# Output product: half of the last pass by split weights, two-bank PSUM tiles, and a set order of transposes and norms

## The chip, the cores and the metric

The kernel runs on one core of one Trainium2 chip. The metric is device time in microseconds for one execution. The kernel before was timed in three runs: 2250.57, 2253.21 and 2257.24 us, median 2253.21.

## The reference

A trunk of two layers works on an input of 1024 tokens with 1024 features, all in float32. Layer 0 mixes with attention, layer 1 with a gated recurrence. Behind each mixer stand an output projection with a norm and a residual, and then a gated feed-forward product:

```python
def rmsnorm(x, g):
    xf = x.astype(jnp.float32)
    y = xf * lax.rsqrt(jnp.mean(xf * xf, axis=-1, keepdims=True) + RMS_EPS)
    return (y * g.astype(jnp.float32)).astype(x.dtype)

def swiglu(h, w_gate, w_up, w_down):
    return (jax.nn.silu(h @ w_gate) * (h @ w_up)) @ w_down

    for layer in range(DEPTH):
        ...
            m = attention_mixer(h, attn_w_in[j], attn_rel_bias[j], attn_w_out[j])
        ...
        x = x + rmsnorm(m, norm_mix_post[layer])
        h = rmsnorm(x, norm_ffn_pre[layer])
        f = swiglu(h, ffn_w_gate[layer], ffn_w_up[layer], ffn_w_down[layer])
        x = x + rmsnorm(f, norm_ffn_post[layer])
```

The mixer ends with a product by `w_out` (1024 x 1024). That product, `norm_mix_post`, the residual, `norm_ffn_pre` and the start of the gate product are what this case is about.

## The kernel before

Most products run in float32r on operands split into a high part and the rest (`hi`, `lo`): three products hi x hi, lo x hi and hi x lo are added in PSUM. A product of plain float32 operands, without a split, is one instruction that shows as two records in the trace.

The output product `out_product` runs once per layer. It takes the 1024 tokens in eight tiles of 128. The weights are eight blocks (`kt`) of 128 x 1024. Tiles 0 to 2 are the first pass and tiles 3 to 5 the second: for each `kt` the weights are loaded, split by ScalarE (hi) and VectorE (lo), the activations likewise, and each tile gets 2 halves x 3 products of 128 x 512. Tiles 6 and 7 are the last pass: all eight weight blocks are loaded again into the eight buffers with the tag `w`, and used plain, with plain activations (16 instructions per tile).

Behind a tile's product stands its chain of small steps, in `post_norm`, `rstd` and `pre_norm`: VectorE multiplies the PSUM halves by the gain into `mg` (L223); ScalarE squares the halves into `junk` with a sum (L175); GpSimd adds the two sums (L177), scales and adds epsilon (L178) and raises to -0.5 (L179); VectorE forms the new residual `x` (L226); ScalarE squares it, GpSimd works out its factor, ScalarE scales `x` into `mg` (L200); TensorE transposes it in eight instructions (L208); and `HiddenS.take` copies the two PSUM tiles (ScalarE, L85), forms four differences `tf` (VectorE, L89) and splits everything into `hS` (ScalarE hi, L96; VectorE lo, L89).

The feed-forward's gate and up products (`gate_up`) use Strassen's scheme: seven products per block with combinations of weight quarters (A11, A12, A22, S1 to S4, held split in `q`) and combinations of the transposed activations (`hS`). A token tile fills 64 of the 512 columns of `hS` (`cols` in `HiddenS.take`). The first gate block is computed in two halves of the columns: `early`, 0 to 256, which tiles 0 to 3 fill, and `late`, 256 to 512, which tiles 4 to 7 fill. Each half has 7 x 4 x 3 = 84 products of 128 x 256 (L549 to L551). The first up product, with 512 columns, follows.

The order on each engine is found when the kernel is built: a scheduler with estimated times takes the instruction that is ready first, within what the buffers of the pools allow. `tc.issue_after(i)` keeps an instruction behind another in that order. DMAs are issued by SP in its own order; a DMA waits there for its buffer. PSUM has eight banks of 512 float32 per partition: six single-bank tiles (`mm`) and two for transposes (`tr`).

## Time and profile before

| | |
|---|---|
| median of three runs | 2253.21 us |
| profiled execution, own time | 2252.08 us |
| its span on the core | 2250.3 us |
| mean granted TensorE clock | 0.992 of 2.4 GHz |
| TensorE, VectorE, ScalarE, GpSimd busy | 98%, 68%, 51%, 10% |
| output product, layer 0: first product, last pass, first up product | 511.15, 580.09, 640.55 us |
| output product, layer 1: last pass, first up product | 1558.68, 1616.98 us |

Times are counted from the start of the span. The profile gives each engine's busy time; because matmuls are pipelined, a record of a matmul is longer than the distance to the next one, so costs on TensorE are read from start to start. "Idle before" is the time in which the engine had nothing running ahead of an instruction, with the instruction that ended it. A wait on an engine other than TensorE costs only if TensorE waits for it later.

### The profile page before, as it was taken

The page shows a single profiled execution, that of the slowest core. Times are in us where ns is not written, and L with a number is a line of the kernel's source. Part 1 is how long each engine was busy: PE and PEld are TensorE (multiplying, and loading weights), DVE is VectorE, ACT ScalarE, POOL GpSimd, SP SyncE. Part 2 cuts the span into 40 slices and gives each one's busy share as a digit, 9 for nine tenths or more (in the row PEclk, how much of TensorE's full clock was granted, in tenths as well). Part 3 has the DMA queues.
Part 4 walks back from the last instruction along what each step waited for, and adds up shares of the span by engine and source line. Part 5 has one row for each costly group of instructions (what it writes and reads, how often), then busy time and mean ns, then how long its engine had stood idle before and what let it go on. Part 6 is the DMA issues. An engine that isn't in the chain of part 4 may idle for free. (4 is left out here: it accounts for less than half of the span.)

```text
span 2250.3 us, 30764 instructions
## 1 busy us (share of the span) xinstructions
PE 2204.5 (98%) x11166; PEld 1804.5 (80%) x11166; DVE 1537.2 (68%) x2504; ACT 1146.9 (51%) x2132; POOL 220.5 (10%) x474
## 2 busy tenths in 40 slices
PE   8999999999999999999999999999999999999997
PEld 8888888878678888888887777887788888888875
DVE  5776765464677767676867677436887767769665
ACT  4545455465765454432536576537755454425433
POOL 2111212131100000000001232102000000000010
PEclk9999999999999999999999999999999999999998
DMA  5101011125623323245558511358233323337466
GB/s 171 44 29 34 24 43 46 55 98 156 223 85 113 116 90 122 89 131 183 173 157 255 141 57 47 95 183 273 71 117 108 122 90 116 96 117 264 130 206 187
DMA packets 187132, 273.13 MB, mean 121 GB/s; under 512 B 13922, under 2 KB 115298, under 8 KB 186979
## 3 DMA queue, kind: packets, MB, share of 16 engines
q1 hardware_dynamic: 186338, 269.06, 38.1%
q10 hardware_dynamic: 640, 2.10, 0.3%
q8 instruction: 88, 1.44, 0.3%
q14 instruction: 66, 0.53, 0.1%
HBM read 205.57 MB, written 65.54 MB: 120 GB/s over the span
## 5 line engine op out<-in xcount | busy, mean ns | idle before, releaser
L549 PE MATMUL ps<-hS,q 128*128 128x512 f32 (+1 forms) x1288 | 490.5, 382 | 3.0 <-ACT hS L96 2.9
L550 PE MATMUL ps<-hS,q 128*128 128x512 f32 (+1 forms) x1288 | 490.6, 381 | 0.2 <-DVE hS L89 0.2
L551 PE MATMUL ps<-hS,q 128*128 128x512 f32 (+1 forms) x1288 | 489.1, 381 | 0.0
L530 DVE TENSOR_TENSOR q<-raw,q 128x512 fp32r<-128x512 f32 x308 | 204.4, 686 | 180.8 <-ACT q L529 180.4
L549 PEld LDWEIGHTS ps<-hS,q 128*128 128x128 f32 x1288 | 242.8, 189 | 50.1 <-ACT hS L96 4.1
L550 PEld LDWEIGHTS ps<-hS,q 128*128 128x128 f32 x1288 | 243.7, 189 | 47.2 <-DVE hS L89 0.7
L551 PEld LDWEIGHTS ps<-hS,q 128*128 128x128 f32 x1288 | 243.6, 189 | 45.8
L529 ACT CAST q<-raw 128x512 fp32r<-128x512 f32 x308 | 176.9, 615 | 157.3 <-DVE raw L538 137.1
L630 PE MATMUL ps<-o,o 128*128 128x512 f32 x616 | 241.2, 392 | 2.4 <-DVE o L625 2.3
L631 PE MATMUL ps<-o,o 128*128 128x512 f32 x616 | 238.6, 392 | 0.5 <-DVE o L741 0.5
L629 PE MATMUL ps<-o,o 128*128 128x512 f32 x616 | 222.0, 395 | 8.9 <-ACT o L740 5.9
L518 ACT ACTIVATE raw<-raw,gcol 128x256 f32<-128x256 f32 x352 | 150.2, 498 | 157.2 <-DMA raw<-in_ffn_w_up_dram 83.1
L624 ACT CAST o<-raw 128x512 fp32r<-128x512 f32 x206 | 123.9, 621 | 197.2 <-PE ps L631 60.5
L625 DVE TENSOR_TENSOR o<-raw,o 128x512 fp32r<-128x512 f32 x206 | 137.9, 688 | 66.2 <-ACT o L624 65.2
L178 POOL TENSOR_SCALAR rs<-ss 128x1 f32<-128x1 f32 x64 | 30.2, 472 | 1266.5 <-ACT junk L175 1169.1
L629 PEld LDWEIGHTS ps<-o,o 128*128 128x128 f32 x616 | 116.4, 189 | 37.7 <-ACT o L740 8.0
L155 DVE TENSOR_TENSOR wlo<-raw,whi 128x1024 fp32r<-128x1024 f32 x76 | 92.9, 1223 | 67.5 <-ACT whi L154 66.4
L630 PEld LDWEIGHTS ps<-o,o 128*128 128x128 f32 x616 | 116.4, 189 | 28.0 <-DVE o L625 3.9
L631 PEld LDWEIGHTS ps<-o,o 128*128 128x128 f32 x616 | 116.3, 189 | 24.9 <-DVE o L741 0.9
L154 ACT CAST whi<-raw 128x1024 fp32r<-128x1024 f32 x76 | 79.8, 1052 | 53.0 <-PE ps L166 20.2
L369 ACT COPY pt<-tr 128x512 f32<-128x512 f32 (+1 forms) x128 | 65.5, 527 | 78.9 <-PE tr L365 78.3
L165 PE MATMUL psq<-hT,whi 128*128 128x512 f32 x256 | 101.2, 395 | 1.1 <-DVE v L264 1.1
(194 smaller groups left out, 4281.1 us busy)
## 6 DMA issues: line engine op xcount, KB each, us to landing
raw<-in_ffn_w_down_dram SPq DMA_DIRECT2D x96, 256.0 KB, 4.3
raw<-in_ffn_w_gate_dram SPq DMA_DIRECT2D x44, 512.0 KB, 4.2
raw<-in_ffn_w_up_dram SPq DMA_DIRECT2D x44, 512.0 KB, 4.4
gS<-c SPq DMA_DIRECT2D x88, 256.0 KB, 3.7
raw<-gS SPq DMA_DIRECT2D x88, 256.0 KB, 2.9
gA<-c SPq DMA_DIRECT2D x66, 256.0 KB, 3.3
raw<-in_attn_w_in_dram SPq DMA_DIRECT2D x24, 512.0 KB, 4.1
raw<-in_attn_w_out_dram SPq DMA_DIRECT2D x24, 512.0 KB, 4.2
```

The costliest lines, as they stand in the source:

```text
L165: nc.tensor.matmul(ps, wh[:, kt, cols], hh[:, kt, :], start=kt == 0, stop=False)
L518: nc.scalar.activation(raw[:, i], raw[:, i], AF.Copy, scale=gain[:, 4 * k + i:4 * k + i + 1])
L529: self.last = nc.scalar.copy(t[:, 0], src).ins
L530: nc.vector.tensor_tensor(t[:, 1], src, t[:, 0].bitcast(F32), op=ALU.subtract)
L549: nc.tensor.matmul(ps, a[:, 0, kt, :], bh, start=kt == 0, stop=False)
L550: nc.tensor.matmul(ps, a[:, 0, kt, :], bl, start=False, stop=False)
L551: nc.tensor.matmul(ps, a[:, 1, kt, :], bh, start=False, stop=kt == 3)
L624: nc.scalar.copy(t[:, 0], src)
L625: tt(t[:, 1], src, t[:, 0].bitcast(F32), op=ALU.subtract)
L629: nc.tensor.matmul(ps, a[0], b[:, 0], start=first, stop=False)
L630: nc.tensor.matmul(ps, a[0], b[:, 1], start=False, stop=False)
L631: nc.tensor.matmul(ps, a[1], b[:, 0], start=False, stop=last)
```

## The change

Six things change, all around the output product of both layers.

- In the last pass the split weights of the last four `kt` of the second pass are kept (`kept`), and tiles 6 and 7 are multiplied by them with split activations, in three products each. Only the first four `kt` are loaded again and used plain. Their `w` buffers are those of the kept weights.
- A tile's product stands in one PSUM tile of two banks (three such buffers), so that the gain product, and the square, are one instruction of 1024 elements. Transposes have a pool of their own, and the feed-forward opens its pool behind the output product.
- `rstd` scales by D^-0.5 within the square; the sums of two parts are chained, so that GpSimd has one instruction fewer behind the last square.
- `post_norm` is cut in two: for each of the first two passes the three gain products and squares are issued first, then the rest of each tile.
- The transposes and takes of tiles 3 to 7 are put in a set order by `behind`, that is by `issue_after`.
- The first gate block's weights are loaded and split from within the output product, in another order (A22 third); the last three splits, S3, S1 and S4, stand behind the norm of tile 6. Products S2 and A22 of the early half stand behind the transposes of tiles 6 and 7.

```diff
         ss = [pool.tile([P, 1], F32, tag="ss", bufs=4, name=self.uid("ss")) for _ in parts]
-        for p, o in zip(parts, ss):
-            self.squared = nc.scalar.activation(junk, p, AF.Square, accum_out=o).ins
-        if len(parts) == 2:
-            nc.gpsimd.tensor_tensor(ss[0], ss[0], ss[1], op=ALU.add)
-        nc.gpsimd.tensor_scalar(rs, ss[0], 1.0 / D, EPS, op0=ALU.mult, op1=ALU.add)
+        eps = EPS
+        for i, (p, o) in enumerate(zip(parts, ss)):
+            self.squared = nc.scalar.activation(junk, p, AF.Square, scale=D ** -0.5, accum_out=o).ins
+            if i < len(parts) - 1:
+                nc.gpsimd.tensor_scalar(o, o, eps, None, op0=ALU.add)
+                eps = o
+        nc.gpsimd.tensor_scalar(rs, ss[-1], eps, None, op0=ALU.add)
         nc.gpsimd.tensor_tensor(rs, rs, self.neghalf, op=ALU.pow)
...
+    @contextmanager
+    def behind(self, instructions):
+        with ExitStack() as c:
+            for i in instructions:
+                c.enter_context(self.tc.issue_after(i))
+            yield
...
-            nc.scalar.activation(h, x, AF.Copy, scale=rs)
+            self.scaled = nc.scalar.activation(h, x, AF.Copy, scale=rs).ins
...
+                self.turned[t] = nc.tensor.transpose(
+                    ps[:, j * P:(j + 1) * P], h[:, kt * P:(kt + 1) * P], self.ident).ins
             pst.append(ps.rearrange("p (a b) -> p a b", a=4))
+        if later:
+            return lambda: sink.take(t, pst, h, pool)
         sink.take(t, pst, h, pool)
...
+    def post_norm_of(self, ms, mg, x_src, x_dst, t, gpost, sink, pool, x=None):
         nc = self.nc
-        x = pool.tile([P, D], F32, tag="nx", bufs=2, name=self.uid("x"))
+        if x is None:
+            x = pool.tile([P, D], F32, tag="nx", bufs=2, name=self.uid("x"))
         for d, s in rows(t, x_src):
             self.load(x[d, :], s)
         junk = pool.tile([P, D // len(ms)], BF16, tag="junk", bufs=1, name=self.uid("junk"))
         if mg is ms[0][1]:
             rs = self.rstd(pool, [m for _, m in ms], junk)
         for c, m in ms:
-            nc.vector.tensor_tensor(mg[:, c], m, gpost[:, c], op=ALU.mult)
+            scaled = nc.vector.tensor_tensor(mg[:, c], m, gpost[:, c], op=ALU.mult).ins
         if mg is not ms[0][1]:
             rs = self.rstd(pool, [m for _, m in ms], junk)
-        nc.vector.scalar_tensor_tensor(x, mg, rs, x, op0=ALU.mult, op1=ALU.add)
-        for k, (d, s) in enumerate(rows(t, x_dst)):
-            (nc.scalar if k and sink is None else nc.sync).dma_start(s, x[d, :])
-        if sink is not None:
-            self.pre_norm(pool, x, mg, None, sink, t, self.psum_t)
+        self.last_m = [self.squared, scaled]
+        def rest(later=False):
+            nc.vector.scalar_tensor_tensor(x, mg, rs, x, op0=ALU.mult, op1=ALU.add)
+            for k, (d, s) in enumerate(rows(t, x_dst)):
+                (nc.scalar if k and sink is None else nc.sync).dma_start(s, x[d, :])
+            if sink is not None:
+                return self.pre_norm(pool, x, mg, None, sink, t, self.psum_t, later)
+        return rest
...
+        def psum():
+            return pp.tile([P, D], F32, tag="mm", bufs=3, name=self.uid("ps"))
         def matmuls(ps, passes, first, last):
             for n in range(2):
                 for i, (x, y) in enumerate(passes):
-                    nc.tensor.matmul(ps[n], x, y[:, n, :], start=first and i == 0,
+                    nc.tensor.matmul(ps[:, n * 512:(n + 1) * 512], x, y[:, n, :], start=first and i == 0,
                                      stop=last and i == len(passes) - 1)
         def norm(t, ps):
             mg = ap.tile([P, D], F32, tag="mg", bufs=3, name=self.uid("mg"))
-            ms = [(slice(i * 512, (i + 1) * 512), p) for i, p in enumerate(ps)]
-            self.post_norm(ms, mg, x_src, x_dst, t, gpost, sink, ap)
-        gpost = None
+            x = self.apool.tile([P, 1152], F32, tag="first", name=self.uid("x"))[:, :D] if t in (2, 5) else None
+            return self.post_norm_of([(slice(0, D), ps)], mg, x_src, x_dst, t, gpost, sink, ap, x)
+        def split_act(a, ah, al):
+            nc.scalar.copy(ah, a)
+            nc.vector.tensor_tensor(al, a, ah.bitcast(F32), op=ALU.subtract)
+        gpost, kept = None, []
         for t0 in (0, 3):
-            pst = [[self.psum() for _ in range(2)] for _ in range(3)]
+            pst = [psum() for _ in range(3)]
             for kt in kts:
-                pool, bufs = (self.apool, 1) if t0 == 0 and kt == kts[0] else (ap, 3)
-                a = act(kt, t0, 3, pool, bufs)
+                if t0 == 0 and kt == kts[0]:
+                    a, ah, al = self.apool.tile([P, 1152], F32, tag="first", name=self.uid("first")).rearrange(
+                        "p (a b) -> a p b", a=3)
+                    ah, al = ah.bitcast(F32R), al.bitcast(F32R)
+                    nc.sync.dma_start(a, aT[kt][:, 0:3 * P])
+                else:
+                    a = act(kt, t0, 3, ap, 3)
+                    ah, al = (ap.tile([P, 384], F32R, tag=n, bufs=3, name=self.uid(n)) for n in ("ah", "al"))
                 wh, wl = self.split(wv[kt], 2, 512)
-                ah, al = (pool.tile([P, 384], F32R, tag=n, bufs=bufs, name=self.uid(n)) for n in ("ah", "al"))
-                nc.scalar.copy(ah, a)
-                nc.vector.tensor_tensor(al, a, ah.bitcast(F32), op=ALU.subtract)
+                kept = kept[-3:] + [(wh, wl)]
+                split_act(a, ah, al)
                 for t in range(3):
                     tok = slice(t * P, (t + 1) * P)
                     matmuls(pst[t], [(ah[:, tok], wh), (ah[:, tok], wl), (al[:, tok], wh)],
                             kt == kts[0], kt == kts[-1])
             if gpost is None:
                 gpost = self.gain(ap, "gpost", gpost_v)
-            for t in range(3):
-                norm(t0 + t, pst[t])
+            rests = [norm(t0 + t, pst[t]) for t in range(3)]
+            for rest in rests[:2]:
+                rest()
+            take = rests[2](t0 > 0)
+        pst = [psum() for _ in range(2)]
+        for i, (kt, (wh, wl)) in enumerate(zip(kts[4:], kept)):
+            a = act(kt, 6, 2, ap, 3)
+            ah, al = (ap.tile([P, 384], F32R, tag=n, bufs=3, name=self.uid(n))[:, :2 * P] for n in ("ah", "al"))
+            split_act(a, ah, al)
+            for t in range(2):
+                tok = slice(t * P, (t + 1) * P)
+                matmuls(pst[t], [(ah[:, tok], wh), (ah[:, tok], wl), (al[:, tok], wh)], i == 0, False)
         rows, acts = [], []
-        for i, kt in enumerate(kts):
+        for i, kt in enumerate(kts[:4]):
             raw = self.main.tile([P, 2, 512], F32, tag="w", bufs=8, name=self.uid("raw"))
             nc.sync.dma_start(raw, wv[kt])
             rows.append(raw)
-            acts.append(act(kt, 6, 2, ap, 3, ("act", "ah", "al")[i % 3]))
+            acts.append(act(kt, 6, 2, ap, 3, ("act", "act", "act", "ah")[i]))
+        turned = {(0, 0): 3, (0, 2): 4, (1, 0): 5}
         for t in range(2):
-            ps = [self.psum() for _ in range(2)]
-            for i in range(KT):
-                matmuls(ps, [(acts[i][:, t * P:(t + 1) * P], rows[i])], i == 0, i == KT - 1)
-            norm(6 + t, ps)
-    def gate_up(self, ap, hS, wg, wu, gain, gO):
...
+        for name, tag in zip(("A11", "A12", "A22", "S2", "S3", "S1", "S4") if behind else
+                             ("A11", "A12", "S2", "S3", "S1", "S4", "A22"), tags):
...
+        with self.behind(behind):
             split("S3", a21)
             split("S1", a22)
             tt(a12, a12, a11, op=ALU.subtract)
             split("S4", a12)
-            return q
+        return q
...
+            with self.behind([self.turned[6]] if first else ()):
+                p6 = product(new(), q["S2"], 4, cols)
+            tt(u2, p6, s1, op=ALU.add)
             tt(s1, p2, s1, op=ALU.add)
...
+            with self.behind([self.turned[7]] if first else ()):
+                p4 = product(new(), q["A22"], 6, cols)
+            tt(u3, u3, p4, op=ALU.subtract)
...
+        def first(l, behind):
+            qg[:] = [self.gate_load(None, io["ffn_w_gate"][l], self.gcol[:, l], 0, ["w"] * 7, behind=behind)]
+            return self.last, self.last_lo
...
-            with pool("o0", "right") as ap:
-                self.out_product(ap, oT,
+            with pool("o0", "right") as ap, psum("po0") as pp:
+                self.out_product(ap, pp, lambda *a: first(0, *a), oT,
```

The order of TensorE in layer 0, before: the transposes of tile 4 (`pst_6341`), the end of tile 7's product (`ps_6504` and `ps_6505` are its halves) and the first early gate product (`ps_6676`).

```order
L462 MATMUL ps_6505<-raw_6425,act_6427 128x512
L462 MATMUL ps_6504<-raw_6429,act_6431 128x512
L208 MATMUL pst_6341<-ident,mg_6319 128x128 x4
L208 MATMUL pst_6346<-ident,mg_6319 128x128 x4
L462 MATMUL ps_6505<-raw_6429,act_6431 128x512
L462 MATMUL ps_6504<-raw_6433,act_6435 128x512
L462 MATMUL ps_6505<-raw_6433,act_6435 128x512
L462 MATMUL ps_6504<-raw_6437,act_6439 128x512
L462 MATMUL ps_6505<-raw_6437,act_6439 128x512
L549 MATMUL ps_6676<-hS_5636,q_6650 128x256
L550 MATMUL ps_6676<-hS_5637,q_6650 128x256
```

Tile 5 is transposed later, among the early products. After, the same place; `ps_6367` and `ps_6368` are the two-bank tiles of tiles 6 and 7, `pst_6326` and `pst_6357` the transposes of tiles 4 and 5, and `pst_6483` those of tile 6:

```order
L491 MATMUL ps_6367<-raw_6449,act_6451 128x512 x2
L491 MATMUL ps_6367<-raw_6453,act_6455 128x512 x2
L220 MATMUL pst_6357<-ident,mg_6277 128x128 x4
L220 MATMUL pst_6362<-ident,mg_6277 128x128 x4
L491 MATMUL ps_6368<-raw_6441,act_6443 128x512 x2
L491 MATMUL ps_6368<-raw_6445,act_6447 128x512 x2
L491 MATMUL ps_6368<-raw_6449,act_6451 128x512 x2
L491 MATMUL ps_6368<-raw_6453,act_6455 128x512 x2
L220 MATMUL pst_6483<-ident,mg_6465 128x128 x4
L220 MATMUL pst_6488<-ident,mg_6465 128x128 x4
L621 MATMUL ps_6681<-hS_5636,q_6526 128x256
```

Tile 6's transposes, which stood behind 38 early instructions, now stand ahead of all of them (`ps_6681` is the first). The second early product, 12 instructions later, writes `ps_6695`, whose bank is the upper one of `ps_6368`.

On TensorE again, where tile 7 is transposed, before (`pst_6544`; `ps_6761` is the last early product, `ps_6779` the first late one):

```order
L549 MATMUL ps_6761<-hS_5640,q_6656 128x256
L550 MATMUL ps_6761<-hS_5641,q_6656 128x256
L551 MATMUL ps_6761<-hS_5640,q_6656 128x256
L208 MATMUL pst_6544<-ident,mg_6522 128x128 x4
L208 MATMUL pst_6549<-ident,mg_6522 128x128 x4
L549 MATMUL ps_6779<-hS_5636,q_6650 128x256
```

and after (`pst_6569`; `ps_6723` is an early product, S1):

```order
L622 MATMUL ps_6723<-hS_5641,q_6530 128x256
L623 MATMUL ps_6723<-hS_5640,q_6530 128x256
L621 MATMUL ps_6723<-hS_5640,q_6530 128x256
L220 MATMUL pst_6569<-ident,mg_6551 128x128 x4
L220 MATMUL pst_6574<-ident,mg_6551 128x128 x4
L622 MATMUL ps_6723<-hS_5641,q_6530 128x256
```

Tile 7's transposes have come forward: in layer 0 they stand behind 43 of the 84 early instructions, and in layer 1 behind 52, where before all 84 were ahead of them.

ScalarE in layer 0, before, from the two squares of tile 6 (`junk_6462`) to the scaling of tile 6 (`mg_6459`); `mg_6319` is tile 4, `q` are gate weights:

```order
L175 ACTIVATE junk_6462,ss_6466<-ps_6441 128x512
L529 CAST q_6656<-raw_6644 128x512
L175 ACTIVATE junk_6462,ss_6467<-ps_6442 128x512
L85 COPY mg_6319<-pst_6341 128x512
L175 ACTIVATE mg_6459,ss_6476<-x_6460 128x1024
L85 COPY mg_6319<-pst_6346 128x512
L529 CAST q_6652<-raw_6638 128x512
L529 CAST q_6653<-raw_6638 128x512
L529 CAST q_6654<-raw_6644 128x512
L96 CAST hS_5636<-mg_6319 128x8x64
L96 CAST hS_5638<-mg_6319 128x4x64
L200 ACTIVATE mg_6459<-x_6460,rs_6475 128x1024
```

After, from the square of tile 6 (`junk_6468`) to its scaling (`mg_6465`); `mg_6277` is tile 5 and `tf_6338` the differences of tile 4:

```order
L178 ACTIVATE junk_6468,ss_6471<-ps_6367 128x1024
L85 COPY mg_6277<-pst_6357 128x512
L85 COPY mg_6277<-pst_6362 128x512
L593 CAST q_6530<-raw_6514 128x512
L96 CAST hS_5640<-tf_6338 128x16x64
L593 CAST q_6531<-raw_6520 128x512
L96 CAST hS_5636<-mg_6277 128x8x64
L96 CAST hS_5638<-mg_6277 128x4x64
L178 ACTIVATE mg_6465,ss_6478<-x_6466 128x1024
L593 CAST q_6532<-raw_6520 128x512
L212 ACTIVATE mg_6465<-x_6466,rs_6477 128x1024
```

The square of tile 6's residual (`x_6460` before, `x_6466` after) had one instruction between tile 6's second square and itself, and now has seven: two copies of tile 5, two casts of gate weights, the cast of tile 4's differences and two casts of tile 5. On VectorE the gain product of tile 7 has likewise moved behind all subtractions of tile 5.

## Rows read from the trace of the kernel before

**Rows 1.** The busy time of each engine on the page: us, share of the span, instructions.

```profile
PE 2204.5 (98%) x11166; PEld 1804.5 (80%) x11166; DVE 1537.2 (68%) x2504; ACT 1146.9 (51%) x2132; POOL 220.5 (10%) x474
```

**Rows 2.** The list of TensorE's waits over the whole span: the waiting instruction, what released it, then us in total, how often, and the longest in us.

```profile
PE pst L208 <- ACT mg L200: 5.1, 2, 2.9
PE ps L549 <- ACT hS L96: 2.9, 3, 1.4
```

**Rows 3.** The timeline of TensorE in layer 0, the first product of the second pass, then from the second pass into the last (start us, us, engine, line, operation, tile, in brackets the idle time before and what ended it).

```profile
548.65 0.50 PE L462 MATMUL ps<-whi,ah 128*128 128x512 f32 x1 [0.47 <-ACT junk L175]
...
570.56 0.39 PE L462 MATMUL ps<-whi,ah 128*128 128x512 f32 x1
...
579.86 0.39 PE L462 MATMUL ps<-whi,al 128*128 128x512 f32 x1
580.09 13.89 PE L462 MATMUL ps<-raw,act 128*128 128x512 f32 x32
593.82 1.04 PE L208 MATMUL pst<-ident,mg 128*128 128x128 f32 x8
594.69 9.61 PE L462 MATMUL ps<-raw,act 128*128 128x512 f32 x22
```

**Rows 4.** The same timeline, the transposes of tiles 6 and 7 and the start of the late gate products.

```profile
615.45 1.14 PE L208 MATMUL pst<-ident,mg 128*128 128x128 f32 x8 [0.58 <-ACT mg L85]
...
625.02 1.71 PE L208 MATMUL pst<-ident,mg 128*128 128x128 f32 x8 [2.92 <-ACT mg L200]
628.06 0.80 PE L549 MATMUL ps<-hS,q 128*128 128x256 f32 x2 [1.32 <-ACT hS L96]
```

**Rows 5.** The same timeline in layer 1, the start of the last pass, the first and last of 27 early products in a row, the transposes of tile 7 and the start of the late products.

```profile
1558.68 1.88 PE L462 MATMUL ps<-raw,act 128*128 128x512 f32 x4
...
1589.96 0.28 PE L550 MATMUL ps<-hS,q 128*128 128x256 f32 x1
...
1593.06 0.28 PE L549 MATMUL ps<-hS,q 128*128 128x256 f32 x1
...
1601.98 1.09 PE L208 MATMUL pst<-ident,mg 128*128 128x128 f32 x8 [2.14 <-ACT mg L200]
1604.50 0.51 PE L549 MATMUL ps<-hS,q 128*128 128x256 f32 x2 [1.43 <-ACT hS L96]
```

**Rows 6.** The timeline of TensorE where the first up product starts, layer 0 and layer 1 (the first row with 512 columns after the late products).

```profile
640.55 0.40 PE L549 MATMUL ps<-hS,q 128*128 128x512 f32 x1
...
1616.98 0.40 PE L549 MATMUL ps<-hS,q 128*128 128x512 f32 x1
```

**Rows 7.** Busy time of each engine in a stretch (us from the start of the span; the number after the last engine is TensorE's granted clock, 1.00 being 2.4 GHz, then the DMA share and GB/s), layer 0 and then layer 1.

```profile
622.00:624.00 2.00, 0.10 (x1) 0.00 (x0) 2.00 (x6) 1.80 (x4) 0.93 (x2) 1.00 0.63 262
624.00:626.00 2.00, 0.98 (x6) 0.98 (x7) 2.00 (x5) 0.99 (x2) 0.00 (x0) 0.84 0.00 0
626.00:632.00 6.00, 4.68 (x21) 4.05 (x20) 4.66 (x10) 3.02 (x5) 0.00 (x0) 0.50 0.00 1
...
1604.00:1606.00 2.00, 1.27 (x5) 1.07 (x6) 1.29 (x3) 1.71 (x3) 0.00 (x0) 0.74 0.00 0
1606.00:1608.00 2.00, 2.00 (x12) 2.00 (x11) 1.97 (x4) 0.00 (x0) 0.00 (x0) 0.50 0.00 0
```

**Rows 8.** Groups by line and shape between 500 and 645 us (tiles, shapes, count, then busy us and mean ns of one, then idle time before and its releasers).

```profile
L462 PE MATMUL ps<-raw,act 128*128 128x512 f32 x64 | 28.0, 592 | 0.0
...
L223 DVE TENSOR_TENSOR mg<-ps,g 128x512 f32<-128x512 f32 x16 | 10.4, 687 | 0.6 <-PE ps L462 0.4
L226 DVE SCALAR_TENSOR_TENSOR x<-mg,rs,x 128x1024 f32<-128x1024 f32 x8 | 10.3, 1282 | 14.5 <-POOL rs L179 7.7 <-DMA x<-in_x_dram 6.8
L89 DVE TENSOR_TENSOR hS<-tf,hS 128x1024 fp32r<-128x1024 f32 x8 | 9.8, 1223 | 2.1 <-ACT hS L96 2.1
L179 POOL TENSOR_TENSOR rs<-rs,neghalf 128x1 f32<-128x1 f32 x16 | 9.6, 598 | 1.3
L175 ACT ACTIVATE junk<-ps 128x512 bf16<-128x512 f32 x16 | 9.5, 593 | 3.0 <-DVE mg L223 2.6
L200 ACT ACTIVATE mg<-x,rs 128x1024 f32<-128x1024 f32 x8 | 9.2, 1145 | 1.1 <-POOL rs L179 1.1
...
L85 ACT COPY mg<-pst 128x512 f32<-128x512 f32 x16 | 8.9, 585 | 1.2 <-PE pst L208 1.2
L175 ACT ACTIVATE mg<-x 128x1024 f32<-128x1024 f32 x8 | 8.5, 1057 | 16.5 <-DVE x L226 16.5
L96 ACT CAST hS<-tf 128x1024 fp32r<-128x1024 f32 x8 | 8.4, 1044 | 3.7 <-DVE tf L89 3.7
...
L178 POOL TENSOR_SCALAR rs<-ss 128x1 f32<-128x1 f32 x16 | 5.8, 361 | 28.5 <-ACT mg L175 27.7 <-POOL ss L177 0.2
```

**Rows 9.** The timeline of ScalarE in layer 0, three casts of gate weights in a row.

```profile
609.92 1.66 ACT L529 CAST q<-raw 128x512 fp32r<-128x512 f32 x3
```

**Rows 10.** DMA issues by line in the window from 560 to 583 us (out<-in, queue, kind, count, KB each, median us from issue to landing).

```profile
raw<-in_attn_w_out_dram SPq DMA_DIRECT2D x9, 512.0 KB, 6.2
act<-oT SPq DMA_DIRECT2D x8, 128.0 KB, 5.7
```

**Rows 11.** The timeline of GpSimd at the end of the kernel, the last tile's norm.

```profile
2242.81 0.19 POOL L177 TENSOR_TENSOR ss<-ss,ss 128x1 f32<-128x1 f32 x1 [3.56 <-ACT junk L175]
2243.09 0.19 POOL L178 TENSOR_SCALAR rs<-ss 128x1 f32<-128x1 f32 x1
```

More of the change, by code (lines that the diff above doesn't have):

```diff
@@ new lines, in out_product @@
+            for i in range(4):
+                with self.behind([self.turned[turned[t, i]]] if (t, i) in turned else ()):
+                    matmuls(pst[t], [(acts[i][:, t * P:(t + 1) * P], rows[i])], False, i == 3)
+            if t == 0:
+                rest = norm(6, pst[0])
+                last_m = self.last_m
+                take6 = rest(True)
+                with self.behind(last_m):
+                    take()
+                order = [self.scaled, sink.last, sink.last_lo]
+        with self.behind([*order, *first(last_m)]):
+            rest = norm(7, pst[1])
@@ L574, in strassen @@
             tt(u2, product(new(), q["S4"], 2, cols), u2, op=ALU.add)
[L575 removed]
+            with self.behind([self.turned[7]] if first else ()):
+                p4 = product(new(), q["A22"], 6, cols)
+            tt(u3, u3, p4, op=ALU.subtract)
         full, early, late = slice(0, 512), slice(0, 256), slice(256, 512)
         for j in range(NF // 2):
[L579 removed]
+            if j:
+                qg = self.gate_load(ap, wg, gain, j, ["w"] * 7, self.last if j == 1 else None)
             if j == 0:
                 first = self.main.tile([P, 4, 256], F32, tag="w", bufs=8, name=self.uid("first"))
[L583 removed]
+                strassen([first[:, i] for i in range(4)], qg, early, True)
                 cg = blocks()
```

98 lines of the change are left out of this document (54 added, 44 removed).

## The prediction

> **What bounds the kernel now.** I read the engines' busy times first: TensorE is busy for 2204.5 of the 2250.3 us, and the next engine, VectorE, for 68% [rows 1]. So an edit pays only where it takes work off TensorE or shortens one of its waits. The list of TensorE's waits shows what the two output products leave: 5.1 us for the scaling of a normalized tile ahead of its transposes, and 2.9 us for a cast of the transposed tile [rows 2]. The timeline places them. In layer 0 the last pass runs without a gap from 580.09 [rows 3]; tile 6's transposes wait 0.58, tile 7's 2.92, and the late gate products 1.32 [rows 4]. In layer 1 the last two are 2.14 and 1.43 [rows 5]. Behind these gaps the granted clock falls from 1.00 to 0.50, from 2.4 to 1.2 GHz: in layer 0 it is 0.84 in 624 to 626 and 0.50 in 626 to 632, which loses 0.16 x 2 + 0.50 x 6 = 3.3 us of TensorE work; in layer 1 0.74 and 0.50, 0.52 + 1.0 = 1.5 us [rows 7]. The mark for each stage is the start of the first up product, 640.55 and 1616.98 [rows 6]: ahead of it are all instructions that the change moves, behind it both kernels have the same order.
>
> **TensorE's own work.** A split product takes (579.86 - 570.56) / 41 = 0.227 us from start to start, a plain fp32 one (593.82 - 580.09) / 16 = 0.858 [rows 3]. Half of the last pass goes from 16 plain products to 48 split ones: 16 x 0.858 = 13.73 becomes 48 x 0.227 = 10.89, so 2.84 us less per layer, all of it on the busiest engine. Transposes keep their count: 0.87 per tile (594.69 - 593.82). An early or late gate product takes 3.10 / 26 = 0.119 [rows 5].
>
> **Between the second and the last pass.** The 0.47 us wait at 548.65 [rows 3] should go, since the norms of three tiles now come first. At the end of pass two the first tile of the last pass takes the PSUM of tile 3, which is ready 12 split products (2.7 us) before. Its gain product of 1024 elements is not in the trace; the nearest rows are two of 687 ns, 1.37 us, and one of 1024 elements from SBUF, 1.22 to 1.28. I take 1.28. The square takes 1.06 [rows 8], with the read of its sum some 1.25. Together 2.5, so there is no wait if both queues are empty, and up to 4 if VectorE first finishes tile 2's four kinds of subtractions. I take 1.0, nearer to the row at 580.09, which shows no gap at all.
>
> **Tile 6.** Its product is now finished before tile 7's plain half begins. From 580.09 - 0.47 + 1.0, through 10.89, two transposes (1.74) and eight plain products (6.86), it ends at 600.1. VectorE still has five subtractions of tile 4, so its gain product starts at about 601.3; square at 602.6, sum and power on GpSimd 0.36 + 0.60 from 603.8, residual on VectorE 1.28 to 606.0 [rows 8]. The next square is queued on ScalarE behind the two copies of tile 5, two gate casts, the cast of tile 4's sums and two casts of tile 5. At 0.58 and 1.04 a piece [rows 8], and 1.66 / 3 = 0.55 for a gate cast [rows 9], that is about 4.0 us from 603.6: the square starts at 607.6 though its input is there at 606.0. Then 1.25, 0.96 on GpSimd and 1.15 for the scaling: transposes at 610.95. TensorE has finished tile 7's product at 579.62 + 1.03 + 10.89 + 3 x 0.87 + 13.73 = 607.9. In the order nothing but the transposes stands there, since all gate products now follow tile 6. New idle time: 3.1 us, where the kernel before had products to run and waited 0.58.
>
> **The second gate product.** Its PSUM is the upper bank of tile 7's two-bank tile. So it waits until tile 7's square is done, and that stands behind tile 7's gain product, which is queued on VectorE behind the last subtractions of tile 5. The square ends at about 616.2. TensorE has then done tile 6's transposes and the 12 products of A11: 610.95 + 0.87 + 1.43 = 613.25. A second new wait of 3.0 us.
>
> **Tile 7.** From 616.2 come 0.96, 1.28, 1.25, 0.96 and 1.15 [rows 8], most in an empty queue: 621.9. In layer 0 there are 31 products in between, 3.7 us, and TensorE waits 1.95 (before 2.92). In layer 1 there are 40, 4.8 us, and it waits 0.9 (before 2.14). Behind the transposes remain 41 and 32 early products, 4.9 and 3.8 us. They cover the copies and casts for which the late products waited 1.32 and 1.43, so those waits go.
>
> **The sum at full clock.** Layer 0: 621.91 + 0.87 + 4.89 + 84 x 0.119 (10.01) = 637.7, 2.9 us sooner than 640.55. Layer 1, with the same steps behind 1558.68 - 0.47: tile 7's transposes at 1600.5, the up product at 1600.5 + 0.87 + 3.81 + 10.01 = 1615.2, 1.8 sooner than 1616.98. One GpSimd instruction less in the kernel's last norm: 0.28 [rows 11]. Other norms have it hidden. Together 5.0.
>
> **The clock.** Two waits of 3 us within 9 us are like those that stand ahead of the fall in rows 7, so I expect one here. What it loses is bounded by nothing and by the second rival's price below; I take the losses of rows 7. Of 3.3 us in layer 0, 1.95 lie in the wait for tile 7; of 1.5 in layer 1, 0.9. That leaves 1.35 + 0.6 = 2.0, and the forecast is 5.0 - 2.0 = 3.0 us less. The profiled execution (2252.08, span 2250.3) lies 1.1 below the median of 2253.21; from the one it makes 2249.1, from the median 2250.2, which I give. [...]
>
> [...] The trace shows the squares ordered behind the gain product (2.6 of their 3.0 us of waiting, [rows 8]); with half tiles the first square could run beside the second product, in two-bank tiles none can. By the rows this lengthens a chain by 1.28 + 1.25 - (0.69 + 0.69 + 0.59 + 0.2) = 0.36, and is in the times above.
>
> **Rivals.** *The new order hides the waits (0.32).* If the scalings come earlier than the queues say, TensorE saves its 2.84 per layer and the waits too. All of 3.1 + 3.0 + 1.95, 3.1 + 3.0 + 0.9 and 2 x 1.0 gone: 17 us, 2231. Half of the seven-microsecond waits gone and no fall of the clock: 7.5 more than 5.0, 2240.7. For it: ScalarE was busy for 51% of the span [rows 1], so what is queued ahead of the square may be done sooner than I let it. Against it: the order on each engine is fixed, and the same walk with the same durations puts the transposes of before at 615.5 and 624.9, where the trace has 615.45 and 625.02 [rows 4].
>
> *The clock stays low (0.09; slower).* If it falls behind the wait for tile 6 and is back only at the late products, layer 0 pays 3.70 - 1.95 for 31 products, 0.87 for the transposes and 4.89 for 41 products, 7.5; layer 1 4.77 - 0.9, 0.87 and 3.81, 8.6. Against the 5.0 it is 11 us slower, 2264. It decides from 5.0 us of loss on. Against it: the fall in layer 1 was over within about 3 us.
>
> *The plain weights come late (0.05; slower).* Their buffers are free only after the first split products of the last pass, 583.4 and 586.1; before, they were loaded during pass two. At 6.2 us to landing [rows 10] they are there at 589.6 to 592.3, and needed from 592.4 on. The residual rows of tiles 6 and 7 are queued on SP behind them and have until 604.8. Each us of landing beyond 9 costs one; slower by over 0.3% takes a loss of (6.8 + 5.0) / 2, some 6 us per layer, 2260.
>
> *It does nothing (0.04).* The late start of the up product is set by the norms, not by the products: 2253.
>
> **From these to the numbers.** What a measurement here can tell is 0.3%, 6.8 us: 2246.4 to 2260.0. The forecast (0.50) with its own bounds holds 2246 to 2256. Faster is the first rival, 0.32; slower the second and the third, 0.14; the rest, 0.54, is within. From 2238 to 2260, 0.12 lie below and 0.08 above.
>
> **What would show it.** Tile 6's transposes with an idle time of some 3 us behind ScalarE's scaling; 12 early products and then a wait for tile 7's square; no wait at the late products; up product 1 to 3 us sooner, counted from the start of the first pass. Wrong if the plain products wait for a DMA, if tile 6's transposes start without a gap (then the first rival), or if the granted clock is 0.50 through all early products.

## The result and the profile after

The changed kernel takes 2259.09 us (median of 20 runs, 2253.01 to 2263.12), the kernel before 2252.81 (20 runs): ratio 1.0025, interval 1.0018 to 1.0032. It is slower by some 6 us, clear of noise. The forecast was 2250.2, faster by 3. The range of 2238 to 2260 holds the time, the direction is wrong, and so is the likeliest case.

TensorE's waits after (waiting instruction, releaser, us in total, times, longest); rows 2 are the same list before:

```profile
PE pst L220 <- ACT mg L212: 8.7, 3, 3.3
PE ps L491 <- ACT junk L178: 6.7, 2, 3.4
```

and of before, beside rows 2, the one that answers to the second:

```profile
PE ps L462 <- ACT junk L175: 0.9, 2, 0.5
```

Where the first was 5.1 us and the second 0.9 there are now 8.7 and 6.7; the wait of the late products for a cast (2.9) is gone. The timeline of TensorE in layer 0, with the first product of the last pass, two of its neighbours, the plain products of tile 7, the transposes of tile 6, the second early product, the transposes of tile 7 and the first up product [rows 3, 4, 6]:

```profile
585.04 0.50 PE L491 MATMUL ps<-whi,ah 128*128 128x512 f32 x1 [3.26 <-ACT junk L178]
...
587.19 0.63 PE L491 MATMUL ps<-wlo,ah 128*128 128x512 f32 x1
587.61 0.63 PE L491 MATMUL ps<-whi,al 128*128 128x512 f32 x1
...
607.17 7.03 PE L491 MATMUL ps<-raw,act 128*128 128x512 f32 x16
617.46 1.97 PE L220 MATMUL pst<-ident,mg 128*128 128x128 f32 x8 [3.25 <-ACT mg L212]
...
622.53 0.39 PE L621 MATMUL ps<-hS,q 128*128 128x256 f32 x1 [1.20 <-ACT junk L178]
...
628.66 1.09 PE L220 MATMUL pst<-ident,mg 128*128 128x128 f32 x8 [2.15 <-ACT mg L212]
...
644.58 0.40 PE L621 MATMUL ps<-hS,q 128*128 128x512 f32 x1
```

The start of the last pass waits 3.26 us where the row at 580.09 had no gap. Two split products behind it lie 0.42 apart, not 0.227, at a granted clock of 0.50 in 587 to 588. Then 3.25 at tile 6, 1.20 at the second early product, 2.15 at tile 7, and none at the late products. Layer 1 [rows 5, 6]:

```profile
1565.32 0.50 PE L491 MATMUL ps<-whi,ah 128*128 128x512 f32 x1 [3.41 <-ACT junk L178]
...
1597.74 1.97 PE L220 MATMUL pst<-ident,mg 128*128 128x128 f32 x8 [3.25 <-ACT mg L212]
...
1602.81 0.58 PE L621 MATMUL ps<-hS,q 128*128 128x256 f32 x1 [0.55 <-ACT junk L178]
...
1624.26 0.40 PE L621 MATMUL ps<-hS,q 128*128 128x512 f32 x1
```

What that makes of the stage (first split product to first up product; it starts at 513.34 and 1493.58) shows in the busy times of before, and then of after, with four short stretches behind the waits (columns as in rows 7):

```profile
511.15:640.55 129.40, 124.01 (x586) 95.42 (x585) 81.22 (x128) 82.69 (x154) 16.98 (x40) 0.97 0.52 171
1489.88:1616.98 127.10, 122.66 (x586) 94.55 (x584) 84.21 (x133) 85.29 (x158) 16.98 (x40) 0.99 0.60 202
```

```profile
513.34:644.58 131.24, 121.37 (x602) 98.27 (x601) 82.89 (x126) 83.04 (x143) 20.84 (x32) 0.97 0.47 152
1493.58:1624.26 130.68, 123.48 (x601) 100.47 (x600) 85.62 (x130) 85.62 (x147) 20.54 (x32) 0.95 0.54 180
585.00:590.00 5.00, 4.96 (x15) 3.93 (x16) 3.92 (x4) 3.84 (x8) 4.15 (x6) 0.66 0.34 131
617.00:625.00 8.00, 6.35 (x40) 6.15 (x41) 5.14 (x8) 4.66 (x9) 0.79 (x2) 0.79 0.22 66
1565.00:1570.00 5.00, 4.68 (x13) 3.70 (x14) 4.19 (x5) 3.85 (x10) 3.95 (x5) 0.66 0.33 128
1597.00:1606.00 9.00, 7.71 (x35) 7.42 (x36) 6.14 (x10) 5.66 (x9) 0.79 (x2) 0.50 0.24 66
```

Layer 0 goes from 129.40 to 131.24: TensorE is busy 2.6 us less (the saved products) and idle 4.5 us more (9.9 against 5.4). Layer 1 goes from 127.10 to 130.68: idle 7.2 against 4.4, and busy 0.8 us more although it has 2.84 us less to do, since its clock in the stage fell from 0.99 to 0.95. Together 5.4 us, the size of the measured loss.

### The profile page after: what moved, and what is told of

Read it like the earlier page. It is cut to its first block, busy times and chain, and to the rows that moved or that the text cites. A ratio compares the mean times of both kernels' runs of the same rounds, so it can differ in the third digit from the quotient of the medians.

```text
span 2256.0 us, 30743 instructions
## 1 busy us (share of the span) xinstructions
PE 2204.9 (98%) x11198; PEld 1814.5 (80%) x11198; DVE 1539.0 (68%) x2496; ACT 1146.3 (51%) x2108; POOL 230.5 (10%) x458
## 4 chain that ended last, share of the span: by engine, by line
PE 80%; DVE 6%; DMA 5%; ACT 4%; issue 3%; POOL 1%; SPq 1%; POOLq 0%; DVEq 0%; ACTq 0%
PE ps L621 12%; PE ps L622 12%; PE ps L623 12%; PE ps L491 4%; PE ps L707 3%; PE ps L708 3%; PE ps L709 3%; PE pso L400 3%; PE tr L391 3%; PE psq L167 3%; PE psq L166 3%; PE psq L168 3%; PE ps L168 2%; PE ps L166 2%; PE ps L167 2%
## 5 line engine op out<-in xcount | busy, mean ns | idle before, releaser
L182 POOL TENSOR_SCALAR rs<-ss 128x1 f32<-128x1 f32 x60 | 39.4, 656 | 1462.8 <-ACT junk L178 1397.7
```

## The experiments

All ratios are to the kernel before, with their intervals. Edits are to the changed kernel unless another is named. Where an edit moved more than its own part, it is said.

**Norms one by one again behind the first pass (e1).** In layer 0 the order from the last pass on is the changed kernel's; in layer 1 tile 7's transposes stand behind 43 early products and not 52.

```diff
-            rests = [norm(t0 + t, pst[t]) for t in range(3)]
-            for rest in rests[:2]:
-                rest()
-            take = rests[2](t0 > 0)
+            if t0 == 0:
+                for t in range(3):
+                    norm(t, pst[t])()
+            else:
+                ...
```

> The changed kernel, with one part undone: behind the first pass each tile's norm is again issued as a whole (tile 0, then 1, then 2) and not three gain products and squares first. The rest of the order, from the last pass on, stays as changed. Theory A: putting three norms first makes tile 0's scaling wait on GpSimd behind the factors of tiles 1 and 2 (in the changed kernel it came 4.5 us after ScalarE was free), so the takes of tiles 0 to 2 end late and the last pass waits 3.3 to 3.4 us for the square of tile 3. Undone, that wait is 0 to 1.0 us in both layers, the fall of the clock behind it goes too, and the time is 6 to 9 us shorter than the changed kernel's: 2250 to 2253 us. Rival B: the wait comes from the two-bank tile, whose square has to follow a gain product of 1024 elements; then it stays at 3 us and the time at 2258 to 2260.

Measured 2255.55, ratio 1.0017 (1.0007 to 1.0027). To see why the changed kernel waits at the last pass, read its GpSimd behind the first pass; L182 is the addition and L183 the power of a norm:

```profile
548.70 1.26 POOL L182 TENSOR_SCALAR rs<-ss 128x1 f32<-128x1 f32 x1 [1.76 <-ACT junk L178]
550.04 1.40 POOL L183 TENSOR_TENSOR rs<-rs,neghalf 128x1 f32<-128x1 f32 x1
551.52 1.32 POOL L182 TENSOR_SCALAR rs<-ss 128x1 f32<-128x1 f32 x1
552.92 0.57 POOL L183 TENSOR_TENSOR rs<-rs,neghalf 128x1 f32<-128x1 f32 x1
553.57 1.32 POOL L182 TENSOR_SCALAR rs<-ss 128x1 f32<-128x1 f32 x1
554.97 0.57 POOL L183 TENSOR_TENSOR rs<-rs,neghalf 128x1 f32<-128x1 f32 x1
```

and VectorE and ScalarE beside it (L250 is the residual, L212 tile 0's scaling):

```profile
548.60 1.28 DVE L250 SCALAR_TENSOR_TENSOR x<-mg,rs,x 128x1024 f32<-128x1024 f32 x1
...
551.47 1.28 DVE L250 SCALAR_TENSOR_TENSOR x<-mg,rs,x 128x1024 f32<-128x1024 f32 x1 [0.46 <-POOL rs L183]
553.52 1.28 DVE L250 SCALAR_TENSOR_TENSOR x<-mg,rs,x 128x1024 f32<-128x1024 f32 x1 [0.77 <-POOL rs L183]
```

```profile
555.57 1.15 ACT L212 ACTIVATE mg<-x,rs 128x1024 f32<-128x1024 f32 x1 [4.50 <-POOL rs L183]
```

The additions at 551.52 and 553.57 start with a residual of 1.28 us and end with it, after 1.32 us; at 557.84 and 558.88, where VectorE is idle, one takes 0.22. Tile 0's factor is third in GpSimd's queue and done at 555.54, so ScalarE idles for 4.50 us. In e1 tile 0's factor comes ahead of tile 1's and nothing is held:

```profile
551.00 0.23 POOL L182 TENSOR_SCALAR rs<-ss 128x1 f32<-128x1 f32 x1 [4.22 <-ACT mg L178]
...
552.00 0.22 POOL L182 TENSOR_SCALAR rs<-ss 128x1 f32<-128x1 f32 x1
```

From there the delay goes through the takes of tiles 0 to 2 to the end of the second pass. In the changed kernel tile 2's last subtraction stands ahead of tile 3's gain product on VectorE, and the square that frees the PSUM follows it. In the kernel before, the same subtraction had ended when tile 3's product did, and the gain product waited for TensorE alone. VectorE before, then VectorE and ScalarE after:

```profile
575.28 1.23 DVE L89 TENSOR_TENSOR hS<-tf,hS 128x1024 fp32r<-128x1024 f32 x1 [0.23 <-ACT hS L96]
576.89 4.09 DVE L223 TENSOR_TENSOR mg<-ps,g 128x512 f32<-128x512 f32 x6 [0.38 <-PE ps L462]
```

```profile
581.48 1.23 DVE L89 TENSOR_TENSOR hS<-tf,hS 128x1024 fp32r<-128x1024 f32 x1 [0.78 <-ACT hS L96]
582.62 3.48 DVE L244 TENSOR_TENSOR mg<-ps,g 128x1024 f32<-128x1024 f32 x3
```

```profile
583.87 1.02 ACT L178 ACTIVATE junk<-ps 128x1024 bf16<-128x1024 f32 x1 [2.43 <-DVE mg L244]
```

In e1 TensorE's waits are:

```profile
PE pst L220 <- ACT mg L212: 12.5, 4, 4.5
...
PE ps L491 <- ACT junk L178: 3.5, 2, 1.7
```

The last pass starts without a wait and at full clock (1.00 in 582 to 590 and in 1560 to 1568): theory A holds for the wait. But the time gained 2 us by the ratios, with intervals that overlap, and not 6 to 9. The stages of e1:

```profile
513.19:643.63 130.44, 121.93 (x602) 99.25 (x601) 84.00 (x130) 83.71 (x144) 16.30 (x32) 0.96 0.48 153
1492.60:1621.39 128.79, 120.19 (x601) 97.70 (x600) 85.94 (x131) 85.73 (x147) 18.38 (x32) 0.97 0.54 183
```

TensorE is idle for 17.1 us in the two, as in the changed kernel (9.87 + 7.20). What went at the last pass came back in two places. The two waits of L491, 1.7 each, stand in the second pass: 18 products run without a wait, and the next needs the PSUM of tile 1, whose square ScalarE now issues behind the square of tile 0's residual (550.82 behind 549.76). (The row at 548.65 [rows 3] is this same place in the kernel before, with 0.47, and not the first product of the pass.) And tile 6's wait grew from 3.25 to 4.4 and 4.5.

**All norms one by one (e2).**

```diff
-            rests = [norm(t0 + t, pst[t]) for t in range(3)]
-            for rest in rests[:2]:
-                rest()
-            take = rests[2](t0 > 0)
+            for t in range(3):
+                rest = norm(t0 + t, pst[t])
+                if t < 2:
+                    rest()
+            take = rest(t0 > 0)
```

> As e1, and tiles 3 to 5 are also normed one by one. Theory A: no further gain at the start of the last pass; what changes is the chain to tile 6, whose transposes wait 3.25 us in the changed kernel. If that wait comes from the queue ahead of tile 6's second square on ScalarE, it changes little (2.5 to 4 us), and the time is within 2 us of e1's. Rival: three norms first is also what delays tile 6; then its wait falls under 1.5 us and the time is 3 to 5 us shorter than e1's.

Measured 2247.05, ratio 0.9982 (0.9973 to 0.9992): faster than before. Tile 6's wait is 2.3, between the two expectations, the gain over e1 8 us, more than either. So three norms first behind the second pass costs more than behind the first, and GpSimd is held there in the same way. The addition beside a residual behind the second pass, in e1 and then one in e2, where it is not held:

```profile
586.80 1.32 POOL L182 TENSOR_SCALAR rs<-ss 128x1 f32<-128x1 f32 x1
...
588.13 0.22 POOL L182 TENSOR_SCALAR rs<-ss 128x1 f32<-128x1 f32 x1
```

By its profile the two stages of e2 are 126.85 each, 5.5 us shorter than e1's together: TensorE is idle 3.7 us less (13.4 against 17.1) and busy 1.8 us less, at a granted clock of 0.99 in both stages against 0.96 and 0.97. The order of the takes and of the early products, which the scheduler sets, moved with this edit too.

**Early products in two-bank tiles (e3), and with e2 (e4).** Two early products share one tile, and the first two take a free one. The feed-forward opens its own PSUM pool behind the early products.

```diff
-                return self.psum()[:, :cols.stop - cols.start]
...
+                if not halves:
+                    two = pp.tile([P, D], F32, tag="mm", bufs=3, name=self.uid("ps"))
+                    halves.extend([two[:, 0:512], two[:, 512:1024]])
+                return halves.pop(0)[:, :cols.stop - cols.start]
```

> The changed kernel, with the early gate products written into the same two-bank PSUM tiles as the output product, two products to a tile, so that the first two take the banks of tile 4 or 5 and not one of tile 7's. They may then run ahead of tile 6's transposes. Theory A (the waits at tiles 6 and 7 are paid because no product can be put into them, and the second product waits for tile 7's square): tile 6's wait falls from 3.25 to under 1 us, the wait for tile 7's square (1.2 and 0.55) goes, and so does part of the half clock behind them; the wait of 3.3 at the start of the last pass stays. Time 5 to 10 us shorter than the changed kernel's: 2249 to 2254. Rival: the chain of norms to tile 7 alone sets the late products; then filling the gaps earlier only moves the idle time to tile 7's transposes, and the time is within 2 us of 2259.

> e2 and e3 together. If the two costs are apart (theory A for both) they add: 2240 to 2247 us, faster than the kernel before (2252.8). If the chain to tile 7 sets the end whatever happens ahead of it, no better than the better of the two.

e3: 2260.45, ratio 1.0039 (1.0028 to 1.0051). e4: 2249.23, 0.9991 (0.9982 to 1.0001). The early products did move ahead of tile 6, and the wait for tile 7's square went. But with few buffers the later ones wait for VectorE to read their pairs; of e3:

```profile
PE pst L220 <- ACT mg L212: 3.8, 2, 1.9
PE ps L621 <- DVE first L655: 3.7, 2, 1.9
```

The idle time moved, as the rival said. e4 is no better than e2.

**The residual in two halves (e5).**

```diff
-            nc.vector.scalar_tensor_tensor(x, mg, rs, x, op0=ALU.mult, op1=ALU.add)
+            for c in (slice(0, 512), slice(512, D)):
+                nc.vector.scalar_tensor_tensor(x[:, c], mg[:, c], rs, x[:, c], ...
```

> The changed kernel, with the residual x of each post-norm formed by two VectorE instructions of 512 columns and not one of 1024. In the changed kernel GpSimd's addition for a norm takes 1.32 us where it starts beside such an instruction of 1.28, and ends with it, and 0.22 elsewhere. Theory A (GpSimd is held while VectorE runs that instruction): held by one half only, it takes 0.6 to 0.8 us beside it, and the last pass waits 0.5 to 1.5 us less than 3.3. Rival B (that addition is slow for another reason, as its place behind ScalarE's sums): it stays at 1.3 and the wait at 3.3. Time 2255 to 2260 in both; the durations decide.

GpSimd of e5 behind the first pass:

```profile
546.12 0.73 POOL L182 TENSOR_SCALAR rs<-ss 128x1 f32<-128x1 f32 x1 [1.76 <-ACT junk L178]
546.93 0.92 POOL L183 TENSOR_TENSOR rs<-rs,neghalf 128x1 f32<-128x1 f32 x1
547.94 0.70 POOL L182 TENSOR_SCALAR rs<-ss 128x1 f32<-128x1 f32 x1
```

The addition takes 0.70 to 0.73 beside halves, and 0.78 to 0.79 behind the second pass: theory A. The power behind it now takes 0.92 beside the second half, against 0.57, so the sum of both is 1.65 against 1.89, and little is won. The last pass waits 1.65 and 2.31, tile 6 5.4 to 6.0, and the time is 2264.26 (two runs, 1.0051, 1.0031 to 1.0072), over what both expected. The test shows that the addition's time follows the length of the residual beside it (0.70 and 0.73 against 1.32); it does not settle how much of the loss is that hold and how much the place of tile 0's factor in the queue.

**Without the kept weights (e6), and the kept weights alone on the kernel before (e7).**

```diff
-        for i, (kt, (wh, wl)) in enumerate(zip(kts[4:], kept)):
-            ...
-        for i, kt in enumerate(kts[:4]):
+        for i, kt in enumerate(kts):
```

> The changed kernel without the kept weights: all eight weight blocks of the last pass are loaded again and used plain (32 instructions per layer), all else as changed. Forecast of the sum: 2.84 us of TensorE per layer come back, so the stage is 5.7 us longer: 2263 to 2266 us. Rival: the start of the tile 6 and 7 norms sets the end, and the longer products hide the waits at the last pass and at tile 6 (2 x 3.3 and 2 x 3.25); then the time is within 2 us of the changed kernel's 2259 or under it.

> The kernel before with the kept weights alone: four weight blocks of the last pass as split products, four plain; single-bank tiles, norms one by one, the order left to the scheduler. Forecast of the sum: 5.7 us of products go, and if no wait takes their place 2246 to 2248 us. Theory A (norms in sequence cost no wait at the last pass): the last pass starts with less than 1 us of wait; tiles 6 and 7 come out together behind the early products, and the late products wait for tile 6 and 7, 2 to 4 us per layer, so 2249 to 2253. Rival: no gain at all or slower than before, because the plain weights are late.

e6: 2260.33, ratio 1.0033 (1.0019 to 1.0047), by the ratio 2 us over the changed kernel; the intervals don't tell 0 from 5. In the profiled executions its stages are 133.04 and 134.41, 5.5 us longer, but the execution profiled took 2264.03, more than the other four. Tile 6's transposes wait no more; the second early product, which needs the bank of tile 7, waits 5.5 and 5.3 in their place. e7: 2251.75 (one of its ten times is 2731.25), 0.9995 (0.9985 to 1.0006), in the range of theory A. There TensorE is busy 3.1 and 0.3 us less than before and idle 1.8 and 2.0 more, with tile 7's transposes waiting 3.6 in each layer. The saved products alone make no measurable difference: they finish sooner and wait for the same norms.

**Tile 7's norm not held back (e8 on the changed kernel, e9 on e2), and issued ahead of the gate splits (e10 on e2).**

```diff
-        with self.behind([*order, *first(last_m)]):
-            rest = norm(7, pst[1])
+        split7 = first(last_m)
+        rest = norm(7, pst[1])
```

In e10 the two new lines stand the other way round, with `last_m` taken between them, so that S3, S1 and S4 stand behind the norm of tile 7 and not of tile 6.

> The changed kernel without the constraint that sets tile 7's norm behind tile 6's scaling, tile 5's take and the gate splits S3, S1 and S4; the order there is the scheduler's, which puts tile 7's gain product ahead of the last split and of half of tile 5's subtractions. Theory C (the set order makes tile 7's norm late, and with it the second gate product, whose bank it holds, and the end of the stage): the second product no longer waits for tile 7's square (1.2 and 0.55 before), tile 7's transposes come 2 to 4 us sooner after the stage's start (115.3 and 115.9 in the changed kernel), and the time is 3 to 7 us shorter, 2252 to 2256. Rival D (VectorE and ScalarE have more work than fits between the last pass and the late products, whatever its order): what moves ahead displaces other work, and the time stays within 2 us of 2259.

> e2 (all norms one by one, 2247) without that same constraint. Theory C: tile 7's transposes come 2 to 3 us sooner than e2's 111.8, time 2242 to 2245. Rival D: 2246 to 2249.

> e2 with tile 7's norm issued ahead of the first gate weights' splits in the program, so that the splits S3 and S1 come behind its gain product. Theory C: tile 7's gain product some 2 us sooner than in e9, time 2240 to 2244, unless the third or fourth gate product then waits for its split weights. Rival D: those products wait for their splits by as much, and the time is 2246 to 2249.

e8: 2251.13, 0.9996 (0.9985 to 1.0007). e9: 2244.20, 0.9966 (0.9952 to 0.9980). e10: 2240.82, 0.9949 (0.9933 to 0.9965). Tile 7's gain product (L244) on VectorE in the changed kernel, in e8 and in e10:

```profile
618.97 1.23 DVE L89 TENSOR_TENSOR hS<-tf,hS 128x1024 fp32r<-128x1024 f32 x1 [1.11 <-ACT hS L96]
620.11 1.22 DVE L244 TENSOR_TENSOR mg<-ps,g 128x1024 f32<-128x1024 f32 x1
```

```profile
615.53 1.21 DVE L244 TENSOR_TENSOR mg<-ps,g 128x1024 f32<-128x1024 f32 x1
```

```profile
611.41 1.23 DVE L244 TENSOR_TENSOR mg<-ps,g 128x1024 f32<-128x1024 f32 x1 [0.52 <-PE ps L491]
```

In the changed kernel tile 7's product is done at 614.0 (607.17 + 8 x 0.858), and its gain product starts at 620.1, behind the whole take of tile 5. In e8, whose stage starts at 510.72, it comes 2.0 us sooner after the start of the stage (104.8 against 106.8), though tile 7's product ends 1.8 us later there; in e10 it waits for TensorE and no queue, 1.2 us sooner after the start of the stage than in e9 (98.9 against 100.0), where 2 were expected. Nothing waits for a late split. Theory C holds: the waits that go in e8 are the two that the forecast named, the second product's and tile 7's, 3.9 us over both layers; TensorE's idle time as a whole falls by 2.2 (14.8 against 17.1). The ratios put the gain at 7 us; in the profiled execution the two stages (129.13 and 128.57) are 4.2 us shorter. But tile 7's transposes in e8 come only 0.1 and 1.1 us sooner after the start of the stage than the 115.3 and 115.9 of the changed kernel, against the 2 to 4 expected, and in e9 0.1 and 1.6 sooner than in e2, against 2 to 3: more early products now stand ahead of them in TensorE's order, 59 of 84 in layer 0 of e8 against 12 + 31 in the changed kernel, so the products run in what was idle time.

**Two closing runs on e10: without kept weights (e11), and with three norms first (e12).** The edits are those of e6 and, the other way, of e2.

> e10 without the kept weights (all eight weight blocks of the last pass loaded again and plain), all else as in e10. If the saved products count once the waits are gone, the 2 x 2.84 us of the forecast's sum come back: 2245 to 2248 us against e10's 2240.8. Rival: the chain of norms still sets the transposes of tiles 6 and 7, the longer products only fill its waits, as in the changed kernel where the same step cost 1.2; then 2240 to 2243.

> The changed kernel with tile 7's norm issued ahead of the first gate weights' splits as in e10, but the three norms first kept in both passes. If the two orders cost apart, the three norms first cost what lies between e10 and this one: 5 to 8 us, so 2246 to 2249, with a wait of 3.3 to 3.7 us at the last pass and of 2 to 3.3 at tile 6. Rival: with tile 7's norm early nothing else matters, 2240 to 2243.

e11: 2242.88, 0.9960 (0.9946 to 0.9974). e12: 2250.73, 0.9995 (0.9986 to 1.0005). The stages of e10, then of e11:

```profile
512.55:635.27 122.72, 118.74 (x603) 95.77 (x601) 81.60 (x125) 83.25 (x143) 14.19 (x32) 1.00 0.50 163
1483.35:1605.93 122.58, 118.44 (x601) 95.65 (x600) 85.04 (x130) 85.67 (x147) 16.27 (x32) 1.00 0.57 192
```

```profile
510.40:635.88 125.48, 121.81 (x586) 92.90 (x585) 80.76 (x122) 81.28 (x139) 14.31 (x32) 1.00 0.56 176
1484.81:1610.16 125.35, 121.68 (x585) 92.79 (x584) 84.12 (x127) 83.49 (x143) 16.39 (x32) 1.00 0.61 204
```

They differ by 2.76 and 2.77 us, the 2.84 of the sum, at a clock of 1.00 in all four. The timed ratios differ by 0.0011, some 2.5 us, with intervals that allow 0 to 7, and e11's time lies in the range of its rival; so the size rests on the profiles. e12 costs 10 us against e10 by the ratios, where 5 to 8 were expected, and 8.4 by the stages (126.35 and 127.31); the last pass waits 3.4 and 3.6, tile 6 2.1 in both layers, as expected. With tile 7's norm early, three norms first still costs.

## Why the prediction was wrong

**What held.** The products saved: 2.84 per layer forecast, 2.8 in e10 against e11. Tile 6's wait: 3.1 forecast, 3.25 measured in both layers, behind the scaling and no other instruction. That it fits is in part luck: tile 6's product ended 4.0 us later than forecast, and the queues had that time to empty. In e1, where it ended 3.2 us sooner than in the changed kernel, the wait was 4.4, with VectorE reaching tile 6's gain product 2.7 us behind the product's end; the changed kernel took 1.6, the forecast 1.2. The second early product starts 5.07 us after tile 6's transposes; forecast 5.3 (613.25 + 3.0 - 610.95), as 2.3 us of work and 3.0 of waiting. It came as 3.9 and 1.2, since the transposes and about half of the 12 products ran at a granted clock of 0.50 (617 to 620; 0.80 in 620 to 621). Tile 7's transposes follow tile 6's by 11.2 and 11.7 us, forecast 11.0. The late products wait for nothing. The plain weights were never waited for.

**The step that failed** is the first one, "Between the second and the last pass": three norms first was counted as a gain of 0.47 us at the second pass and a wait of 1.0 at the last. The gain came. The wait was 3.26 and 3.41, at the upper end (4) that the forecast had worked out from VectorE finishing tile 2 first and then set aside because the kernel before showed no gap there. That row could not bear this out: in the kernel before tile 2's take had ended when tile 3's product did (576.51, gain product at 576.89), and the change moved the takes. The norms behind the first pass were not walked at all, and elsewhere the walk gave GpSimd 0.36 + 0.60 per factor wherever it stood; three norms first puts the additions beside the residuals, where they take 1.32, and tile 0's factor behind those of tiles 1 and 2 (e1). With the norms one by one in both passes (e2) the time is 0.0043, some 10 us, shorter than the changed kernel's, more than the whole loss.

**What hung on it.** A fall of the clock that the forecast did not have there: 0.66 in 585 to 590 and in 1565 to 1570, 1.7 us each. The forecast put tile 6's transposes 99.8 us after the stage's start and they came at 104.1: 2.3 for the wait and 1.7 for the clock are 4.0 of the 4.3. Twice that would be 8 of the 8.6 us between a forecast of 3.0 less and a loss of 5.6 (0.0025 x 2253). But this is the account of one trace, and not what a repair gives back: in e1, without that wait and that fall, tile 6's transposes still came at 102.1 and 102.0, and only 2 us of time were won. So tile 6's chain was sized too small as well: from the end of tile 6's product to its transposes the forecast had 10.9 us, e1 has 12.3.

**The clock behind tile 6.** Forecast as a net loss of 2.0 with 1.95 and 0.9 hidden in waits; measured 8 x 0.21 = 1.7 in layer 0 and 9 x 0.50 = 4.5 in layer 1, against 3.3 and 1.5 of rows 7 before. Layer 1 is where the second rival's mechanism, a clock that stays low, was partly true: it costs 3 us there. The clock is read as the share that the trace gives; no run shows its rate in GHz, and no step of the sum uses it. As a whole the result is no rival's; the slower side came from a wait that had been sized too small.

**The size of tile 7.** That the norm of tile 7 stands behind tile 5's take was read from the order and priced. What it is worth was not: 0.0029 to 0.0033 of the time, by the changed kernel against e8 (1.0025 to 0.9996) and by e2 against e10 (0.9982 to 0.9949); by the stages 4.2 and 8.4 us. Of the change's parts, the kept weights gain 5.5 us in the end, by the profiles, three norms first costs 8 to 10 (e10 against e12, the changed kernel against e2) and the place of tile 7's norm 4 to 8. Either of the two, undone alone, takes away the loss (e2, e8). In the changed kernel these don't add without rest: undone behind the first pass alone, three norms first gave back only 2.

**Open.** How three norms first divides into the hold on GpSimd and the order of its queue: a factor worked out on another engine would tell, and was not tried. What the two-bank tiles cost is open too, since no run of the change undoes them: with norms one by one the wait in the second pass is 1.7 in two-bank tiles (e1, e2, e10) and 0.47 in the single-bank tiles of the kernel before, where the forecast had priced the longer chain at 0.36. Behind the second pass of layer 0 the first square starts 0.72 us behind the start of its tile's first gain product before (577.61, 576.89), beside the second one, and 1.25 behind the start of the whole one after (583.87, 582.62), at its end.

The best version is e10: the change with norms one by one and tile 7's norm ahead of the gate splits, 0.9949 of the kernel before (0.9933 to 0.9965).

## What to carry to other kernels

When a change issues several chains' first steps together, write down the queue of every engine in the chains, the small ones too: in the changed kernel GpSimd served the first factors of tiles 1 and 2 (548.70, 551.52) ahead of tile 0's second (553.57), and ScalarE idled 4.50 us. A bound that comes from a queue is not refuted by a row of the kernel before, if the change moves what stands in that queue. An order set by hand should hold back only work that somebody is known not to wait for; test each such line by taking it out.

## What the runs showed of the hardware

In the changed kernel GpSimd's addition of 128 x 1 takes 0.22 us where VectorE is idle (557.84 and 558.88), and 1.32 beside a residual of 128 x 1024 that takes 1.28 (551.52 and 553.57). Beside halves of that instruction it takes 0.70 and 0.73 behind the first pass (e5). The prediction had priced each norm's addition as if nothing held it.

In the changed kernel the clock fell behind a wait with TensorE busy again: at the start of the last pass of layer 0 TensorE worked on after 3.26 us of waiting, was busy for 4.96 of the five microseconds from 585 on, and had a granted clock of 0.66 in them.
